# Four-kilobyte pieces for the gate and up weights of a mixture-of-experts layer

## The chip, the core and the metric

The kernel runs on one core of one Trainium2 chip. The metric is the device time of one execution in microseconds (us), as the median of several runs. The core has five engines that each run their own instruction stream in order: TensorE (PE, matrix products; its weight loads are listed apart as PEld), VectorE (DVE), ScalarE (ACT), GpSimd (POOL) and SyncE (SP), which here issues nearly all the transfers from memory. The transfers are carried by 16 DMA engines.

## The reference

256 tokens of width 1024 pass through three layers, all in float32: a layer with forgetting attention and sparse attention, then a mixture of experts, then two hybrid layers (a gated recurrence beside windowed attention). The change is in the mixture of experts:

```python
hid = silu(einsum('td,edf->etf', t, w_gate)) * einsum('td,edf->etf', t, w_up)
hid = hid * combine.T[:, :, None]          # top 2 of 16 experts for each token
y = einsum('etf,efd->td', hid, w_down)
```

There are 16 experts; for each, w_gate and w_up are 1024 x 512 and w_down is 512 x 1024, so 2 MB each.

## The kernel before

The instructions are made by Python generators, and a scheduler in the kernel puts them in an order for each engine before anything runs. It has a cost model of its own (for a DMA: bytes over 360 bytes per ns plus a constant, so the number of bytes counts and not their arrangement) and picks, engine by engine, the task that its model says can start first. Where the model says that PE would stand idle, `keep_warm` puts matmuls on a tile of ones into PE's stream; they write a PSUM tile that nobody reads (`warm` in the rows). They are in the stream once and for all: they run whether or not PE would have had to wait on the chip.

Weights arrive through `loader`. It walks `K.plan`, a list of 1 MB units, takes a free slot (`raw`, 128 partitions x 2048 floats) for each, and lets SP issue its DMAs; at most `K.raw_max` slots are out at a time (`MOE_RAW` = 19 in the expert part). Units of the other layers are then split by ACT and DVE into two halves of lower precision; the expert weights are used as they are (`how == "whole"`).

`plan_moe` makes for each expert four units "gu", each with two chunks of 128 rows of w_gate and the same two of w_up, and two units "d" of w_down. Row number k * 128 + p of the weights lies in partition p, so a partition of a gu unit receives four separate pieces of 512 floats: two of w_gate, two of w_up, side by side with a gate row beside an up row.

`moe` runs one expert after the other. Each expert has room for 64 tokens (`CAP`). For every four experts, `group(q)` gathers their tokens: a matmul per chunk k of 128 columns, with those columns of the tokens as the stationary operand and a 0/1 matrix `Pm` (tile `rows`) as the moving one, gives the chunk's transposed tokens; ACT or DVE scales them by the norm gains `K.gT` into `xt`. The first group (q = 0) takes the tokens `K.x` in full float32. For the other three, `halves()` has split `K.x` once into two parts, `xhl` (tiles `xh` and `xl`): ACT copies the upper part, DVE subtracts. After the gather the expert's eight chunks of gate and up are multiplied (`bank<-raw,xt` in the rows), the product goes through SwiGLU on ACT and DVE (tile `route`), w_down follows (`bank<-raw,route`), and a matmul with the transposed 0/1 matrix (`acc<-rows`) adds the weighted result to the sum for all tokens. `rows_of(e)` makes that transposed matrix: DVE writes two 0/1 tiles (`route<-cp,route`), PE transposes them (`bank<-cp,route`).

`overflow` is a branch that computes all experts for all tokens if some expert has more than 64 tokens; it is not entered with these inputs.

For comparison, one other place reads memory at a distance: `blocks` in the first layer adds a position table to keys of which it reads every 16th element (`cb<-cb`, 64 partitions x 120 elements).

Of the kernel before, what the change touches and what calls it, by code (L numbers as in the profile page):

```python
# [9 lines left out]
F32 = mybir.dt.float32  # L10
# [487 lines left out]
def loader(K, between):  # L498

    nc, sch = K.nc, K.S  # L500
    loaded = [Flag() for _ in K.plan]
    raws = {}

    def load():
        yield ("if", lambda: K.go)
        for i, u in enumerate(K.plan):
            yield ("if", lambda: K.raws < K.raw_max and K.slots.free)
            K.raws += 1
            raw, s = yield from big(K, [128, 2048], "raw")
            rv = raw[:, :u.a * u.n].rearrange("p (a n) -> p a n", a=u.a)  # L510
            for src, c in u.pieces:
                yield nc.sync.dma_start(rv[:, :, c:c + src.shape[2]], src)
            raws[i] = (raw, s, rv)
            loaded[i].done = True
            if i in between:
                yield from between[i]()

    def part(u, i, j, src, sh, w, s):
        wh, wl = (w[:, o:o + sh[0] * sh[1]].rearrange("p (a n) -> p a n", a=sh[0]) for o in (0, 1024))
        yield nc.scalar.activation(wh, src, AF.Copy)  # L520
        yield nc.vector.tensor_sub(wl, src, wh.bitcast(F32))
        u.half[j] = (wh, wl, s)
        u.flag[j].done = True
        if all(f.done for f in u.flag):
            K.raws -= 1
            K.slots.release(raws.pop(i)[1])

    sch.spawn(load(), P_SPLIT)
    for i, u in enumerate(K.plan):
        yield wait(loaded[i])  # L530
        if u.how == "whole":
            u.half = raws.pop(i)
            u.flag[0].done = True
            continue
        rv = raws[i][2]
        for j in range(2):
            yield ("if", lambda: K.halves < K.half_max and K.slots.free)
            K.halves += 1
            w, s = yield from big(K, [128, 2048], "w", F32R)
            if u.how == "col":  # L540
                src, sh = rv[:, :, 128 * j:128 * j + 128], [8, 128]
            else:
                m = u.a // 2
                src, sh = rv[:, m * j:m * j + m, :], [m, u.n]
            sch.spawn(part(u, i, j, src, sh, w, s), P_LATE if u.key[:2] == "wo" else P_SPLIT)
# [171 lines left out]
def split(K, h, l, src):  # L717

    yield K.nc.scalar.activation(h, src, AF.Copy)
    yield K.nc.vector.tensor_sub(l, src, h.bitcast(F32))  # L720
# [583 lines left out]
def plan_moe(K):  # L1304
    I = K.I

    def down(e):
        wr = I["w_down"][0, e].rearrange("(a p) c -> p a c", p=128)
        for u in range(2):
            K.plan.append(Unit("d", [(wr[:, 2 * u:2 * u + 2], 0)], 2, 1024, "whole"))  # L1310
    for e in range(NE):
        for u in range(4):
            wr = [I[nm][0, e].rearrange("(a p) c -> p a c", p=128)[:, 2 * u:2 * u + 2] for nm in ("w_gate", "w_up")]
            K.plan.append(Unit("gu", [(wr[0], 0), (wr[1], 512)], 2, 1024, "whole"))
        if e:
            down(e - 1)
    down(NE - 1)
# [6 lines left out]
def moe(K, edge, done):  # L1324
    nc, I, sch = K.nc, K.I, K.S
    sp = sch.spawn
    ident = K.c("ident")
# [130 lines left out]
    t_half, xhl = [], []  # L1458

    def halves():  # L1460

        for nm in ("xh", "xl"):
            xhl.append((yield from big(K, [128, 2, D], nm, F32R)))
        for t in range(2):
            yield from split(K, xhl[0][0][:, t], xhl[1][0][:, t], K.x[:, t])

    def both(a, b):
        yield wait(a)
# [2 lines left out]
    def group(q):  # L1471

        g = Group()
        p = P_EVAC if q else P_EDGE
        t_one = [sp(one_hot(q, t), p) for t in range(2)]
        g.xt = None
        g.there = [Flag() for _ in range(8)]

        def part(k):
            early = q == 0 and k < 6  # L1480
            yield wait(t_one[0] if early else t_one, t_half if q else None)
            res = K.accs if early and k < 4 else K.banks
            pg, b_ = yield from (acc_tile if res is K.accs else bank)(K, [128, 4, CAP])
            for t in range(2):
                yield wait(t_one[t])
                c = slice(k * 128, k * 128 + 128)
                if q == 0:
                    yield nc.tensor.matmul(pg, K.x[:, t, c], Pm[:, t].bitcast(F32), start=(t == 0), stop=(t == 1))
                for i, x in enumerate(xhl if q else []):
                    yield nc.tensor.matmul(pg, x[0][:, t, c], Pm[:, t], start=(t + i == 0), stop=(t + i == 2))  # L1490
            done_.append(sp(put(k, pg, lambda: res.release(b_)), p))

        def put(k, pg, free):
            yield ("if", lambda: g.xt is not None)
            yield scaled(K, g.xt[:, k], pg, K.gT[:, k:k + 1])
            free()
            g.there[k].done = True
        done_ = []
        ts = [sp(part(k), P_GATHER if q == 0 else p) for k in range(8)]
        g.t_gather = sp(both(ts, done_), p)  # L1500
        if q == 0:
            yield wait(t_mask, edge.tasks)
            K.slots.release(K.s_hh, edge.room[1])
            K.raw_max += 1
        g.xt, g.s_x = yield from big(K, [128, 8, 4, CAP], "xt")
        groups[q] = g
# [61 lines left out]
    for e in range(NE):  # L1568
        q, j = divmod(e, 4)
        if j == 0:  # L1570
            yield ("if", lambda: q in groups)
            g = groups[q]
        t_rows[e] = sp(rows_of(e), P_SIDE)
        pg, b_ = yield from bank(K, [128, 2, 256])
        for u_ in range(4):
            u = take(K, "gu")
            for a in range(2):
                k = 2 * u_ + a
                if j == 0:
                    yield wait(g.there[k])  # L1580
                w = yield from whole(K, u)
                for h in range(2):
                    c = w[:, a].rearrange("p (i f) -> p i f", i=2)[:, :, 256 * h:256 * h + 256]
                    yield nc.tensor.matmul(pg[64 * h:64 * h + 64], g.xt[:, k, j], c, start=(k == 0), stop=(k == 7))
            drop_whole(K, u)
        if j == 3:
            K.slots.release(g.s_x)
            if q < 3:
                sp(group(q + 1), P_EVAC)
        hid[e] = sp(hidden(e, pg, b_), P_EVAC)  # L1590
        if e == 1:
            for i in range(4):
                a = yield from acc_tile(K, [128, 512])
                acc.append(a)
        if e:
            yield from down(e - 1)
            downs[e - 1].done = True
        if e == 2:
            K.raw_max -= 2
            t_half.append(sp(halves(), P_EVAC))  # L1600
        if e == 1:
            K.bounds = sp(bounds(), P_SIDE)
        if e == 10:
            box = []
            yield sch.call(lambda: box.append(nc.real.values_load(
                cmi[0:1, 0:1], min_val=0, max_val=S, skip_runtime_bounds_check_because="a count of tokens")))
            n_max = box[0]
            K.raw_max -= 3
        if e == 12:
            yield wait(groups[3].t_gather)  # L1610
            yield from overflow(K, n_max, combF, comb)
            K.raw_max += 3
        if e == 13:
            K.slots.release(xhl[0][1], xhl[1][1])
            K.raw_max, K.half_max = MOE_END, 8
# [8 lines left out]
def overflow(K, n_max, combF, comb):  # L1624

    tc, nc, I = K.tc, K.nc.real, K.I
# [8 lines left out]
    def body():  # L1635
        with tc.If(n_max > CAP):
# [3 lines left out]
            for k in range(8):  # L1640
                pt = bs[k % 2][0][:, 0:S]
                for t in range(2):
                    nc.tensor.transpose(pt[:, t * 128:(t + 1) * 128], hn[:, t, k * 128:(k + 1) * 128], K.c("ident"))
                nc.vector.tensor_scalar_mul(hT[:, k], pt, K.gT[:, k:k + 1])
            with tc.For_i(0, NE, 1) as e:
                for f in range(4):
                    for i, nm in enumerate(("w_gate", "w_up")):
                        w = raw[:, 1024 * i:1024 * i + 1024].rearrange("p (a c) -> p a c", a=8)
                        nc.sync.dma_start(w, I[nm][0][bass.ds(e, 1), :, f * 128:(f + 1) * 128]
                                          .rearrange("o (a p) c -> p (o a) c", p=128))  # L1650
                        pg = bs[i][0][:, 0:S]
                        for k in range(8):
                            nc.tensor.matmul(pg, w[:, k], hT[:, k], start=(k == 0), stop=(k == 7))
# [402 lines left out]
def tile_kernel(ctx, tc, I, out, parts="am01"):  # L2056
# [20 lines left out]
    def router():  # L2077

        yield ("if", lambda: K.next >= 8 or parts[0] == "m")
        g = I["norm_ffn_g"]  # L2080
        yield nc.gpsimd.dma_start(K.gT, bass.AP(tensor=g.tensor, offset=g.offset, ap=[[1, 128], [128, 8]]))
        yield nc.gpsimd.dma_start(K.w20[:, :, 0:4], I["w_group"][0].rearrange("(a p) c -> p a c", p=128))
        yield nc.gpsimd.dma_start(K.w20[:, :, 4:20], I["w_router"][0].rearrange("(a p) c -> p a c", p=128))
        yield nc.gpsimd.dma_start(K.b20[:, 0:4], bcast_rows(I["b_group"], 4))
# [152 lines left out]
```

## Time and profile before

| | us |
|---|---|
| median of 3 runs (lowest to highest) | 995.18 (995.14 to 996.44) |
| profiled execution, device time | 995.24 |
| its span, first to last instruction | 993.5 |
| PE busy in the span | 979.1 |
| DVE busy | 691.4 |
| ACT busy | 501.2 |
| POOL busy | 28.9 |

The profiled execution is 2 us longer than its span and agrees with the median of the runs. An engine's busy time is an average over very different stages, so it is read by stage: the expert part's first product with expert weights starts 249.5 us into the span and the last one ends near 486 us.

### The profile page before, as it was taken

The numbers are of one execution on the slowest core, as the hardware profiler recorded it, in microseconds if no ns is written. First come the engines' busy times: TensorE is split into PE (matmuls) and PEld (weight loads), VectorE is DVE, ScalarE is ACT, GpSimd is POOL, SyncE is SP. The second block draws the span as 40 slices with busy tenths as digits, with TensorE's granted clock in tenths as the row PEclk, the third lists the DMA queues.
The fourth block names the chain that finished last, engine by engine and source line by source line (L and its number), as shares of the span: only waits on it lengthen the run. The fifth ranks groups of instructions, "written<-read, shape, count | busy, mean of one in ns | idle before, by whom it ended". The sixth has DMA issues, their size and how long they took to land.

```text
span 993.5 us, 16750 instructions
## 1 busy us (share of the span) xinstructions
PE 979.1 (99%) x6385; PEld 750.9 (76%) x6385; DVE 691.4 (70%) x1746; ACT 501.2 (50%) x1070; POOL 28.9 (3%) x67
## 2 busy tenths in 40 slices
PE   9999999999999999999999999999999999999998
PEld 8877999888434343444588989898788898988887
DVE  5778977876355434533687799899858489899952
ACT  5556879842021111110354648687755265867841
POOL 0101000000000000000000000000100000000000
PEclk9999999999999999999999999999999999999999
DMA  8822683798799999999913415432947142443331
GB/s 304 307 69 88 209 304 109 266 343 301 267 393 373 395 392 396 393 386 343 365 36 92 149 58 171 128 125 72 334 129 252 43 128 76 138 129 127 127 107 43
DMA packets 122931, 210.34 MB, mean 212 GB/s; under 512 B 6142, under 2 KB 54512, under 8 KB 122848
## 3 DMA queue, kind: packets, MB, share of 16 engines
q1 hardware_dynamic: 121632, 206.01, 59.2%
q0 software_dynamic: 1216, 3.22, 1.0%
q8 instruction: 52, 0.85, 0.4%
q14 instruction: 31, 0.25, 0.1%
HBM read 208.17 MB, written 1.05 MB: 211 GB/s over the span
## 4 chain that ended last, share of the span: by engine, by line
PE 47%; DVE 6%; DMA 1%; issue 1%; POOL 0%; ACT 0%; DVEq 0%; POOLq 0%
PE acc L202 35%; PE bank L202 11%; DVE ha L202 2%; PE warm L202 1%; DVE ap L202 1%; DMA raw<-in_w_in_dram 1%; DVE hb L202 1%; DVE w L202 1%; DVE og L202 0%; POOL sq L202 0%; DVE tiny L202 0%; DVE x L202 0%; ACT za L202 0%; DVE hn L202 0%; ACT hb L202 0%
## 5 line engine op out<-in xcount | busy, mean ns | idle before, releaser
L202 DVE TENSOR_TENSOR w<-raw,w 128x1024 fp32r<-128x1024 f32 (+1 forms) x196 | 235.3, 1220 | 28.2 <-ACT w L202 27.1
L202 PE MATMUL acc<-hh,w 128*128 128x256 f32 x1280 | 244.2, 287 | 0.0
L202 ACT ACTIVATE w<-raw 128x1024 fp32r<-128x1024 f32 (+1 forms) x196 | 198.7, 1041 | 21.9 <-PE acc L202 11.1
L202 PEld LDWEIGHTS acc<-hh,w 128*128 128x128 f32 x1280 | 201.8, 191 | 3.7 <-issue 1.4
L202 PE MATMUL acc<-hl,w 128*128 128x256 f32 x640 | 184.0, 288 | 0.0
L202 PE MATMUL acc<-w,hh 128*128 128x512 f32 (+2 forms) x512 | 155.2, 380 | 0.0
L202 PEld LDWEIGHTS acc<-hl,w 128*128 128x128 f32 x640 | 122.3, 191 | 3.5 <-issue 1.7
L202 PE MATMUL bank<-raw,xt 128*64 128x512 f32 x512 | 119.4, 600 | 0.0
L202 PEld LDWEIGHTS acc<-w,hh 128*128 128x128 f32 x512 | 92.1, 188 | 16.9 <-issue 2.1
L202 PE MATMUL acc<-w,hl 128*128 128x512 f32 (+2 forms) x256 | 96.5, 377 | 0.0
L202 ACT ACTIVATE route<-bank,route 128x256 f32<-128x256 f32 x16 | 7.6, 474 | 166.2 <-PE bank L202 166.2
L202 PE MATMUL acc<-w,og 128*128 128x512 f32 x384 | 89.1, 391 | 0.0
L202 PEld LDWEIGHTS acc<-w,og 128*128 128x128 f32 x384 | 71.7, 188 | 14.7
L202 PEld LDWEIGHTS bank<-raw,xt 128*64 128x64 f32 x512 | 33.1, 136 | 55.0 <-issue 48.7
L202 DVE TENSOR_TENSOR ha<-ha 128x256 f32<-128x256 f32 (+5 forms) x216 | 71.6, 365 | 4.2 <-PE bank L202 4.0
L202 ACT ACTIVATE ap<-ap,tiny 128x256 f32<-128x256 f32 (+1 forms) x110 | 47.8, 448 | 27.3 <-DVE tiny L202 26.8
L202 PE MATMUL bank<-raw,route 128*64 128x512 f32 x256 | 60.4, 599 | 0.0
L202 PEld LDWEIGHTS warm<-ones 128*128 128x128 f32 x325 | 45.6, 201 | 15.4 <-issue 9.1
L202 PE MATMUL warm<-ones 128*128 128x256 f32 x325 | 54.5, 309 | 2.7 <-ACT ones L424 2.4
L202 PEld LDWEIGHTS acc<-w,hl 128*128 128x128 f32 x256 | 48.3, 189 | 7.3
L202 DVE TENSOR_SCALAR route<-route 128x256 f32<-128x256 f32 (+2 forms) x24 | 6.2, 272 | 57.7 <-ACT route L202 57.6
L202 PEld LDWEIGHTS bank<-raw,route 128*64 128x64 f32 x256 | 16.8, 136 | 28.8 <-issue 25.8
(276 smaller groups left out, 1350.5 us busy)
## 6 DMA issues: line engine op xcount, KB each, us to landing
raw<-in_w_in_dram SPq DMA_DIRECT2D x68, 1024.0 KB, 6.1
raw<-in_w_gate_dram SPq DMA_DIRECT2D x64, 512.0 KB, 10.1
raw<-in_w_up_dram SPq DMA_DIRECT2D x64, 512.0 KB, 10.6
raw<-in_w_down_dram SPq DMA_DIRECT2D x32, 1024.0 KB, 11.9
raw<-in_w_out_dram SPq DMA_DIRECT2D x20, 1024.0 KB, 5.2
raw<-in_cmp_k_w_dram SPq DMA_DIRECT2D x2, 1024.0 KB, 5.8
raw<-in_cmp_v_w_dram SPq DMA_DIRECT2D x2, 1024.0 KB, 5.6
raw<-in_w_fox_up_dram SPq DMA_DIRECT2D x2, 1024.0 KB, 12.2
```

The lines of the kernel that those rows point to most:

```text
L202: go = lambda: f(*a, **k)
```

## The change

Row 8 p + k of w_gate and w_up now lies in partition p as chunk k. Two neighbouring chunks are two neighbouring rows in memory, so a partition of a gu unit receives two pieces of 1024 floats: one of w_gate into the first half of the slot, one of w_up into the second (`how == "pair"`). The product's moving operand takes its 256 gate columns and its 256 up columns at a distance of 1024 floats instead of 512. The tokens' columns must be taken in the same order: chunk k is now every eighth column, starting at k. The first group's gather reads `K.x` so, as its stationary operand; the split writes `xh` and `xl` with the columns already in the new order and reads `K.x` at the distance for it. The gains `K.gT` are loaded in the same order, which makes each partition's eight values neighbours in memory. w_down, the router's weights and everything outside the expert part stay as they are.

```diff
             for src, c in u.pieces:
-                yield nc.sync.dma_start(rv[:, :, c:c + src.shape[2]], src)
+                if u.how == "pair":
+                    yield nc.sync.dma_start(raw[:, c:c + 1024].rearrange("p (a n) -> p a n", a=2), src)
+                else:
+                    yield nc.sync.dma_start(rv[:, :, c:c + src.shape[2]], src)
...
-            wr = [I[nm][0, e].rearrange("(a p) c -> p a c", p=128)[:, 2 * u:2 * u + 2] for nm in ("w_gate", "w_up")]
-            K.plan.append(Unit("gu", [(wr[0], 0), (wr[1], 512)], 2, 1024, "whole"))
+            wr = [I[nm][0, e].rearrange("(p a) c -> p a c", a=8)[:, 2 * u:2 * u + 2] for nm in ("w_gate", "w_up")]
+            K.plan.append(Unit("gu", [(wr[0], 0), (wr[1], 1024)], 2, 1024, "pair"))
...
-            yield from split(K, xhl[0][0][:, t], xhl[1][0][:, t], K.x[:, t])
+            yield from split(K, *(a[0][:, t].rearrange("p (k d) -> p k d", k=8) for a in xhl), K.x[:, t].rearrange("p (d k) -> p k d", k=8))
...
-                    yield nc.tensor.matmul(pg, K.x[:, t, c], Pm[:, t].bitcast(F32), start=(t == 0), stop=(t == 1))
+                    yield nc.tensor.matmul(pg, K.x[:, t, k::8], Pm[:, t].bitcast(F32), start=(t == 0), stop=(t == 1))
...
-                    c = w[:, a].rearrange("p (i f) -> p i f", i=2)[:, :, 256 * h:256 * h + 256]
+                    c = w.rearrange("p i (b f) -> p i b f", b=2)[:, :, a, 256 * h:256 * h + 256]
...
-        yield nc.gpsimd.dma_start(K.gT, bass.AP(tensor=g.tensor, offset=g.offset, ap=[[1, 128], [128, 8]]))
+        yield nc.gpsimd.dma_start(K.gT, bass.AP(tensor=g.tensor, offset=g.offset, ap=[[8, 128], [1, 8]]))
```

The overflow branch's loads and transposes are rewritten in the same way.

The scheduler's order is the same on every engine; only the shapes of the gate and up loads and of the load of `gT` differ. On SP, where the expert weights begin behind the first layer's output weights, the rows stand so (- before, + after):

```order
 L202 DMA raw<-in_w_out_dram 128x4x512 x4
-L202 DMA raw<-in_w_gate_dram 128x2x512
-L202 DMA raw<-in_w_up_dram 128x2x512
-L202 DMA raw<-in_w_gate_dram 128x2x512
-L202 DMA raw<-in_w_up_dram 128x2x512
```

Each of these pairs becomes 128x1024 in its old place; no load has moved. On DVE, around the subtraction that makes `xl`, the rows of before and of the changed kernel are word for word the same:

```order
L202 SCALAR_TENSOR_TENSOR rows<-bank,route,rows 64x512 x2
L202 TENSOR_TENSOR xl<-x,xh 128x1024 x2
L202 TENSOR_SCALAR lbt<-lbt 128x16 x2
L202 TENSOR_SCALAR route<-cp,route 128x128
L202 TENSOR_TENSOR lbt<-lbt 128x16
L202 TENSOR_SCALAR route<-cp,route 128x128
L202 CAST rows<-bank 128x256
```

Nothing moved here either: the two 0/1 tiles of the next expert (`route<-cp,route`) still stand right behind the two subtractions.

## Rows read from the trace of the kernel before

**Rows 1.** The page: span, PE's share, and 40 slices of DMA use and rate
```profile
span 993.5 us, 16750 instructions
...
PE   9999999999999999999999999999999999999998
...
DMA  8822683798799999999913415432947142443331
GB/s 304 307 69 88 209 304 109 266 343 301 267 393 373 395 392 396 393 386 343 365 36 92 149 58 171 128 125 72 334 129 252 43 128 76 138 129 127 127 107 43
```
**Rows 2.** Stretches, from:to and length; busy by engine; PEclk, DMA share, GB/s
```profile
332.00:336.00 4.00, 4.00 (x20) 1.81 (x19) 3.29 (x6) 0.38 (x1) 0.00 (x0) 1.00 1.05 388
340.00:344.00 4.00, 4.00 (x22) 1.26 (x18) 1.26 (x3) 1.31 (x3) 0.00 (x0) 1.00 1.03 408
347.00:353.00 6.00, 6.00 (x32) 2.85 (x30) 2.21 (x7) 0.00 (x0) 0.00 (x0) 1.00 1.05 387
448.00:450.00 2.00, 2.00 (x14) 1.64 (x14) 0.88 (x4) 0.00 (x0) 0.00 (x0) 1.00 0.09 20
```
**Rows 3.** Waits of PE's matmuls, 240 to 500 us: in total, times, longest
```profile
PE bank L202 <- DVE hn L202: 0.7, 1, 0.7
...
PE bank L202 <- PEq L1636: 0.2, 1, 0.2
```
**Rows 4.** PE in order of time: start, length; middle and late experts
```profile
379.33 4.51 PE L202 MATMUL bank<-raw,xt 128*64 128x512 f32 x20
...
392.00 4.51 PE L202 MATMUL bank<-raw,xt 128*64 128x512 f32 x20
...
449.76 1.94 PE L202 MATMUL bank<-raw,xt 128*64 128x512 f32 x8
...
453.93 0.98 PE L202 MATMUL warm<-ones 128*128 128x256 f32 x6
...
467.13 1.94 PE L202 MATMUL bank<-raw,xt 128*64 128x512 f32 x8
469.00 0.50 PE L202 MATMUL warm<-ones 128*128 128x256 f32 x2
469.43 1.94 PE L202 MATMUL bank<-raw,xt 128*64 128x512 f32 x8
```
**Rows 5.** SP's issues in order of time: start, length
```profile
435.25 1.93 SPq L202 DMA_DIRECT2D raw<-in_w_up_dram  x1
448.71 0.38 SPq L202 DMA_DIRECT2D raw<-in_w_gate_dram  x1
```
**Rows 6.** ACT, DVE and PE around the split of the tokens
```profile
289.78 2.01 ACT L202 ACTIVATE xh<-x 128x1024 fp32r<-128x1024 f32 x2
...
291.36 2.36 DVE L202 TENSOR_TENSOR xl<-x,xh 128x1024 fp32r<-128x1024 f32 x2
...
293.79 0.28 DVE L202 TENSOR_SCALAR route<-cp,route 128x128 f32<-128x128 f32 x1
...
294.35 0.33 PE L202 MATMUL bank<-cp,route 128*128 128x128 f32 x1
...
295.62 0.33 PE L202 MATMUL bank<-cp,route 128*128 128x128 f32 x1
```
**Rows 7.** DVE groups by form: count, busy us, mean ns, idle before
```profile
L202 DVE TENSOR_TENSOR w<-raw,w 128x1024 fp32r<-128x1024 f32 x192 | 232.4, 1230 | 26.8 <-ACT w L202 25.8
...
L202 DVE TENSOR_TENSOR cb<-cb 64x120 f32<-64x120 f32 x16 | 5.2, 356 | 0.2
...
L202 DVE TENSOR_TENSOR kv<-kv 128x128 f32<-128x128 f32 x8 | 2.0, 288 | 0.1
```
**Rows 8.** PE in order of time: a gather of the first group, one of the second
```profile
255.16 1.99 PE L202 MATMUL bank<-rows,x 128*128 128x256 f32 x8
...
298.43 0.28 PE L202 MATMUL bank<-rows,xh 128*128 128x256 f32 x1
298.55 0.28 PE L202 MATMUL bank<-rows,xl 128*128 128x256 f32 x1
```

More of the change, by code (lines that the diff above doesn't have):

```diff
@@ L530, in loader @@
         yield wait(loaded[i])
-        if u.how == "whole":
+        if u.how in ("whole", "pair"):
             u.half = raws.pop(i)
@@ L1485, in part @@
                 yield wait(t_one[t])
-                c = slice(k * 128, k * 128 + 128)
+                c = slice(128 * k, 128 * k + 128)
                 if q == 0:
-                    yield nc.tensor.matmul(pg, K.x[:, t, c], Pm[:, t].bitcast(F32), start=(t == 0), stop=(t == 1))
+                    yield nc.tensor.matmul(pg, K.x[:, t, k::8], Pm[:, t].bitcast(F32), start=(t == 0), stop=(t == 1))
                 for i, x in enumerate(xhl if q else []):
@@ L1642, in body @@
                 for t in range(2):
-                    nc.tensor.transpose(pt[:, t * 128:(t + 1) * 128], hn[:, t, k * 128:(k + 1) * 128], K.c("ident"))
+                    nc.tensor.transpose(pt[:, t * 128:(t + 1) * 128], hn[:, t, k::8], K.c("ident"))
                 nc.vector.tensor_scalar_mul(hT[:, k], pt, K.gT[:, k:k + 1])
@@ L1649, in body @@
                         nc.sync.dma_start(w, I[nm][0][bass.ds(e, 1), :, f * 128:(f + 1) * 128]
-                                          .rearrange("o (a p) c -> p (o a) c", p=128))
+                                          .rearrange("o (p a) c -> p (o a) c", a=8))
                         pg = bs[i][0][:, 0:S]
```

## The prediction

> **What bounds the kernel now.** I read the page's slices first. In the expert part (the 12th to the 20th slice lie wholly in it or nearly so) the DMA engines are busy nearly throughout at 343 to 396 GB/s, and PE is at 9 in every slice [rows 1]. Both look like the limit there, so the slices don't decide it. The table of stretches tells which gives way. While w_down arrives in pieces of 4 KB the rate is 408 GB/s; while w_gate and w_up arrive in pieces of 2 KB it is 387 to 388 GB/s, at the same share of busy time [rows 2]. So the longer pieces do move faster, by 5%, and the question is only whether anyone waits for them.
>
> The waits say no. Between 240 and 500 us PE's matmuls waited four times, 0.7 us at most and 0.2 us at least, and none of the four was for a DMA [rows 3]. The order of time says why. In the middle of the part an expert takes PE 12.67 us (379.33 to 392.00) without a gap; near the end it takes 17.37 us (449.76 to 467.13), with matmuls on ones in between [rows 4]. An expert's 6.29 MB take 16.0 us at about 394 GB/s (between the two rates of [rows 2]). So in the middle PE eats a stock of loads that were issued ahead, and near the end PE runs at the slower pace that the scheduler wrote into its stream, whether the data are there or not. The stock never runs out: from 448 to 450 us the DMA engines are 9% busy [rows 2], so the load issued at 435.25 [rows 5] has landed by then, and it is the last expert's second unit of gate and up, which PE reads at 467.13 [rows 4]. That is a lead of at least 17 us; the third unit, issued at 448.71, is read at 469.43. PE's stream is the bound of this part, and it hands each delay on to the end, since none of the four waits is long enough to swallow one.
>
> **The change, part by part.** *The loads.* 64 gate and 64 up DMAs keep their bytes, their place on SP and their semaphores, and go from pieces of 2 KB to 4 KB. The 67.1 MB take 173.0 us of DMA time at 388 GB/s and 164.5 us at 408, so 8.5 us of DMA time go. The cover is complete: a lead that is 17 us or more only grows, and the matmuls on ones stay in the stream. Counted: 0. The loads of the layer behind, which queue behind the last w_down, come at most by a share of that earlier; the splits that use them stand in DVE's and ACT's streams behind work on PE's last products, so again 0.
>
> *The moving operand.* The same two runs of 256 floats per matmul, farther apart. Before, too, the runs lay apart, and 20 passes took 4.51 us wherever they stood together [rows 4]; the passes read the same floats in the same runs, so both ends are 0.
>
> *The gains.* One small load by POOL, hundreds of us before its use: 0.
>
> *The split.* Two ACT copies (2.01 us together) and two DVE subtractions (2.36 us together) now read `x` at a distance of 8 floats [rows 6]. The trace has no such read of a large tile. The nearest row is `cb<-cb`, 120 elements of which one input is read at every 16th float: 356 ns. Plain DVE subtractions and additions give 288 ns for 128 elements and 1230 ns for 1024, so 1.05 ns per element and 153 ns fixed, and 120 plain elements would take 279 ns [rows 7]. The distance costs 77 ns there, 0.64 ns per element; for 1024 elements 0.66 us. From below I bound it by 0 (a read at a distance has no reason to be faster), from above by twice that on both engines. I take 0.66 us per instruction on DVE, and the same on ACT, for which no row exists.
>
> The chain then goes so. ACT's copies end at about 291.5 and 293.1 instead of 290.8 and 291.8; DVE's subtractions, from 291.36 on, run into 295.25 instead of 293.72, so 1.5 us later. Behind them on DVE stand the two 0/1 tiles of the next expert; the first ended at 294.07 (293.79 + 0.28) and PE transposes it at 294.35 [rows 6]. PE, in order, has less than 0.28 us to spare there. It would wait about 1.3 us. The second transpose, at 295.62, moves along and finds its tile ready. With ACT at no extra cost the delay is 1.3 - 0.3 = 1.0 us, with twice the cost on both engines DVE ends near 297.1 and PE waits some 3.1 us. Everything behind on PE (products, ones, the other layers) moves by the same amount, and with them what SP and DVE do, since these wait for PE. Counted: +1.3 us, ends 0 and 3.1.
>
> [...]
>
> *The first gather.* 8 chunks, two token halves, two passes each in float32: 32 weight loads from `x` at a distance of 8 floats. The 8 passes of two chunks take 1.99 us, so about 0.22 us a pass [rows 8]. In the second group a pass with its load follows the one before by 0.12 us (298.43 to 298.55) [rows 8], so a plain load of 128 columns needs no more than 0.12 us and hides behind the pass before it. At DVE's 0.64 ns per element a load grows by 0.08 us to 0.20 us: still hidden, except where a chunk's first load has no pass to hide behind, at most 8 times 0.08 = 0.7 us. I take half, +0.35 us; ends 0 and, with loads at three times 0.12 us, 32 x 0.14 = 4.5 us.
>
> *Sum*, against the profiled execution (span 993.5 us, 995.24 us with what lies around it, 0.06 above the median): 995.24 + 0 + 1.3 + 0.35 = 996.9, and beside the median of 995.18 that is 996.8.
>
> **The rivals.** *The loads were the limit after all.* For it: DMA busy throughout, and its rate is 5% better with long pieces. Then up to 8.5 us would come back: 986.7 us. Against: no DMA among PE's waits, the lead of 17 us, and ones in the stream late in the part.
>
> [...]
>
> *Weight loads at a distance outgrow the passes* (slower). The place is the first gather, 247 to 262 us, where PE has nothing else to do than these passes and the first products. It decides from the point where a load takes more than 0.22 us, so nearly twice a plain one. At three times: 995.2 + 4.5 + 1.3 = 1001.0 us. For it: 128 separate reads per partition, and DVE shows that such reads cost. Against: by DVE's figure a load stays at 0.20 us.
>
> *The long pieces come slower* (slower). A load now takes 4 KB out of every 16 KB of memory, where before it took 256 KB in one run. If the gate and up traffic, two thirds of the 171 us from 275 to 446, took 30% longer, that would be 34 us, less the lead of 17: about 1012 us. It begins to count once the pieces are 15% slower. Against: w_down's 4 KB pieces are the fastest here.
>
> *Reads at a distance cost nothing* (the change does nothing for the time): 995.2 us. For it only that no row has this very shape.
>
> **How the numbers follow.** A measurement of this kernel tells about 0.2%, 2 us, from no change: 993.2 to 997.2 counts as the same. Forecast 0.64, of which I put a bit over a quarter above 997.2, since its two terms have ends of 3.1 and 0.7 us and the middle lies close to that line. Reads at no cost 0.16. Weight loads outgrow the passes 0.10. Loads were the limit 0.05. Long pieces slower 0.05. So faster 0.06 (the first rival and a little scatter), same 0.61 (0.46 of the forecast, 0.15 of the free reads), slower 0.33 (0.18 of the forecast, 0.10 and 0.05). The predicted time is 996.8 us. The range goes from 994.8, the free reads with the scatter of runs, to 999.5, the forecast's upper part and the first steps of outgrown loads; out of it lie the two extreme rivals and about half of the outgrown loads.
>
> **What would show it.** Gate and up stretches at about 408 GB/s and a DMA that idles more around 446 us: the loads step is right. `xl<-x,xh` near 1.9 us instead of 1.2 and `xh<-x` near 1.7, with an idle time of PE ahead of the transpose at 294 us that names DVE's `route`: the split step is right, and from there on the same shift in every stage. The eight passes `bank<-rows,x` still at about 2.0 us: the gather step is right; at 2.5 or more the second rival is. The forecast is wrong if PE's time for an expert changes, if a wait of PE names a DMA, or if the shift at 294 us is gone again at 490 us.

## The result: slower by half a per cent

| | before | changed |
|---|---|---|
| median of 5 runs each, us (lowest to highest) | 996.06 (995.14 to 996.48) | 1001.08 (1000.57 to 1002.03) |
| profiled execution: device time, us | 995.24 | 1002.03 |
| its span, us | 993.5 | 1000.3 |
| mean granted clock of TensorE in the five runs | 1.0 in the profiled one | 0.996 to 0.998 |

The ratio is 1.0053, 95% interval 1.0039 to 1.0067: slower, by more than the 0.2% that a measurement of this kernel tells. The prediction was 996.8 us with a range to 999.5.

The page of the changed kernel, the lines that answer to [rows 1] and the one on packets:

```profile
span 1000.3 us, 16750 instructions
...
PEclk9999999999998999999999999999999999999999
...
GB/s 304 300 72 88 214 294 121 284 330 295 252 393 296 408 409 409 409 382 356 356 25 85 127 85 135 126 123 84 329 154 252 43 127 59 153 127 127 125 107 43
DMA packets 106547, 210.34 MB, mean 210 GB/s; under 512 B 6142, under 2 KB 54512, under 8 KB 106464
```

The transfers did what the change meant: 408 to 409 GB/s in the 14th to 17th slice, where before it was 392 to 396 [rows 1]. But the 13th slice has a granted clock that is not full, and the rate falls to 296 GB/s in the same slice. Stretches of the changed kernel (from:to and length; busy time of PE, PEld, DVE, ACT, POOL; granted clock, DMA share, GB/s), the first two against [rows 2]:

```profile
347.00:353.00 6.00, 6.00 (x30) 1.91 (x28) 2.86 (x6) 1.69 (x4) 0.00 (x0) 1.00 1.03 411
448.00:450.00 2.00, 2.00 (x13) 0.79 (x9) 1.19 (x3) 0.14 (x1) 0.00 (x0) 1.00 0.33 133
...
296.00:299.00 3.00, 1.07 (x5) 0.34 (x5) 2.27 (x6) 0.00 (x0) 0.00 (x0) 0.92 1.02 401
299.00:302.00 3.00, 3.00 (x11) 1.33 (x9) 0.79 (x4) 0.00 (x0) 0.00 (x0) 0.50 0.59 176
302.00:305.00 3.00, 3.00 (x9) 0.75 (x6) 0.37 (x2) 0.17 (x1) 0.00 (x0) 0.50 0.72 283
305.00:310.00 5.00, 5.00 (x30) 3.10 (x31) 1.90 (x5) 2.45 (x6) 0.00 (x0) 0.97 0.60 213
```

From 299 to 305 us TensorE has a granted clock of 0.50, where the kernel before has 1.00 in the same stretches. What it did before shows in its order of time, to be read beside [rows 6] and [rows 8]:

```profile
256.26 2.29 PE L202 MATMUL bank<-rows,x 128*128 128x256 f32 x8
258.48 1.08 PE L202 MATMUL bank<-raw,xt 128*64 128x512 f32 x4
...
294.17 1.94 PE L202 MATMUL bank<-raw,xt 128*64 128x512 f32 x8
298.04 0.33 PE L202 MATMUL bank<-cp,route 128*128 128x128 f32 x1 [1.93 <-DVE route L202]
298.30 1.82 PE L202 MATMUL bank<-raw,xt 128*64 128x512 f32 x4
300.06 0.47 PE L202 MATMUL bank<-cp,route 128*128 128x128 f32 x1
...
301.11 3.68 PE L202 MATMUL bank<-raw,xt 128*64 128x512 f32 x8
304.71 0.58 PE L202 MATMUL bank<-rows,xh 128*128 128x256 f32 x1
...
473.95 1.94 PE L202 MATMUL bank<-raw,xt 128*64 128x512 f32 x8
```

PE waited 1.93 us for DVE's 0/1 tile, as the prediction said it would (it said 1.3). Right behind the wait four passes take 1.82 us, and eight take 3.68 where eight took 1.94 ahead of it. Who was late is on ACT and DVE:

```profile
291.47 4.14 ACT L202 ACTIVATE xh<-x 128x1024 fp32r<-128x1024 f32 x2
...
293.60 4.04 DVE L202 TENSOR_TENSOR xl<-x,xh 128x1024 fp32r<-128x1024 f32 x2 [0.58 <-ACT xh L202]
...
297.71 0.28 DVE L202 TENSOR_SCALAR route<-cp,route 128x128 f32<-128x128 f32 x1
```

ACT's two copies went from 2.01 to 4.14 us, DVE's two subtractions from 2.36 to 4.04 [rows 6], and DVE now also waits for ACT.

Where the 6.8 us of span between the two profiled executions went can be read by setting PE's rows side by side. The first gather starts 0.5 us later (247.13 before, 247.59 after). That is start-up, whose length varies from run to run: in the six experiments below whose scheduler's model is the same, the first gather starts between 247.28 and 249.90 us. The first product behind the split's wait, the transpose, stands at 298.04 instead of 294.35 [rows 6], 3.7 us later: 0.5 of start-up, 1.2 us of gather, 2.0 us of wait. The first pass of the second group's gather stands at 304.71; before, the row is

```profile
298.09 0.39 PE L202 MATMUL bank<-rows,xh 128*128 128x256 f32 x1
```

so it comes 6.6 us later, and the 2.9 us since the transpose are the half clock. From there on the shift hardly moves: 473.95 for the 467.13 of [rows 4] is 6.8, and at the end of the span it is 6.8. In the medians the changed kernel is 5.0 us slower; the profiled execution is the slowest of the five.

### The profile page after: what moved, and what is told of

Its sections match the earlier page's. It is cut to its first block, busy times and chain, and to the rows that moved or that the text cites. A ratio compares the mean times of both kernels' runs of the same rounds, so it can differ in the third digit from the quotient of the medians.

```text
span 1000.3 us, 16750 instructions
## 1 busy us (share of the span) xinstructions
PE 983.8 (98%) x6385; PEld 754.5 (75%) x6385; DVE 693.1 (69%) x1746; ACT 503.4 (50%) x1070; POOL 28.6 (3%) x67
## 3 DMA queue, kind: packets, MB, share of 16 engines
HBM read 208.17 MB, written 1.05 MB: 209 GB/s over the span
## 4 chain that ended last, share of the span: by engine, by line
PE 49%; DVE 6%; issue 0%; POOL 0%; ACT 0%; DVEq 0%
PE acc L202 35%; PE bank L202 12%; PE warm L202 2%; DVE ha L202 2%; DVE ap L202 1%; DVE hb L202 1%; DVE w L202 1%; POOL sq L202 0%; DVE og L202 0%; DVE tiny L202 0%; DVE rows L202 0%; DVE x L202 0%; ACT za L202 0%; DVE hn L202 0%; ACT hb L202 0%
## 5 line engine op out<-in xcount | busy, mean ns | idle before, releaser
L202 PE MATMUL bank<-raw,xt 128*64 128x512 f32 x512 | 121.9, 611 | 0.0
```

The costliest lines, as they stand in the source:

```text
L202: go = lambda: f(*a, **k)
```

## The experiments

Each is the kernel before or the changed one with a small edit. All were timed beside runs of the kernel before on the same chip.

**The loads alone.** The kernel before with the long pieces; gather and split read `x` plainly. The amount of work is the same, but the tokens' columns no longer belong to the weights' rows; the same holds, for some of the experts, of the next two kernels.

```diff
-            yield from split(K, *(a[0][:, t].rearrange("p (k d) -> p k d", k=8) for a in xhl), K.x[:, t].rearrange("p (d k) -> p k d", k=8))
+            yield from split(K, xhl[0][0][:, t], xhl[1][0][:, t], K.x[:, t])
...
-                    yield nc.tensor.matmul(pg, K.x[:, t, k::8], Pm[:, t].bitcast(F32), start=(t == 0), stop=(t == 1))
+                    yield nc.tensor.matmul(pg, K.x[:, t, c], Pm[:, t].bitcast(F32), start=(t == 0), stop=(t == 1))
```

(The diff is against the changed kernel.)

> Only the new arrangement of the gate and up loads and of the products' moving operand is kept; the gather and the split of the tokens read x as before, so the experts get tokens whose columns don't match the weights' rows. My theory (the strided reads of x cost the time, the loads nothing): 995.2 to 996.4 us, the same as the kernel before; PE clock 1.0 throughout; gate and up stretches at about 408 GB/s. Rival (the new loads or the wider distance in the moving operand cost the time): about 1001 us, with PE slower per expert or waiting for a DMA.

Measured: 996.12 us against 995.89, ratio 1.0004 (0.9995 to 1.0013), granted clock 1.0 in the profiled execution. One of the eleven runs took 998.20 us with a mean clock of 0.998; it was not traced. A stretch of gate and up loads that had 388 GB/s [rows 2]:

```profile
332.00:336.00 4.00, 4.00 (x19) 1.70 (x19) 3.46 (x6) 0.38 (x1) 0.00 (x0) 1.00 1.03 407
```

So the pieces of 4 KB move 5% faster and change the time by nothing that can be measured. The loads step of the prediction holds, and the loss lies in the reads of `x`.

**The split plain**, the gather still at a distance (the first half of the diff above alone).

> The changed kernel, but the split reads x plainly, so the parts for the second to fourth group have the old column order. My theory: the wait of 1.9 us at 298 us and the fall of the clock behind it are gone, the slower gather of the first group (1.1 us) stays: 996.3 to 997.5 us, clock 1.0. Rival (the slower gather is the larger part): 1000 us or more.

Measured: 997.08 us, ratio 1.0011 (1.0002 to 1.0020), against the same 995.89. PE of this kernel, the gather and the transpose that waited:

```profile
257.02 2.29 PE L202 MATMUL bank<-rows,x 128*128 128x256 f32 x8
...
296.79 0.33 PE L202 MATMUL bank<-cp,route 128*128 128x128 f32 x1
```

No wait ahead of the transpose and no fall of the clock. Eight passes take 2.29 us instead of 1.99 [rows 8]; there are four such groups of eight, so the gather costs 1.2 us, and that is what the medians show. (The transpose stands 2.4 us later than before: the other 1.2 us are start-up, since the first gather starts at 248.34 instead of 247.13.)

**The gather plain**, the split still at a distance (the second half of that diff alone).

> The changed kernel, but the first group's gather reads x plainly, so the first four experts get the old column order. My theory: PE's wait of about 1.9 us for DVE and the 6.8 us at half clock behind it stay, the gather's 1.1 us go: 999.8 to 1001 us. Rival (gather is the larger part): below 998 us.

Measured: 1000.67 us, ratio 1.0042 (1.0028 to 1.0055). PE of its profiled execution, then the stretches of the same place:

```profile
297.45 0.33 PE L202 MATMUL bank<-cp,route 128*128 128x128 f32 x1 [1.95 <-DVE route L202]
...
299.35 3.55 PE L202 MATMUL bank<-raw,xt 128*64 128x512 f32 x8
```
```profile
299.00:302.00 3.00, 3.00 (x13) 1.10 (x11) 1.16 (x4) 0.00 (x0) 0.00 (x0) 0.54 0.78 273
302.00:305.00 3.00, 3.00 (x17) 1.23 (x13) 0.69 (x2) 1.36 (x4) 0.00 (x0) 0.89 0.59 201
```

The same wait, and again a half clock behind it, here for about half as long as in the changed kernel. The eight runs fall into two sets: three with a mean granted clock of 1.0 took 997.24, 997.46 and 998.49 us, five with 0.996 to 0.998 took 999.98 to 1001.84. One program, one order, the same data: in the first set the time is above the kernel before by about the length of the wait (997.46 less 995.89 is 1.6), in the second by 2.5 to 4.4 us more. Only one of the eight was traced, so where the clock fell in the other four, and how often, is not shown. The median of the five, 1001.57, is 5.7 us above the kernel before, more than the changed kernel's 5.0 although the gather's 1.2 us are not in it; the price of the falls varies by more than the gather costs.

**The wait filled.** The changed kernel with 16 matmuls on ones in PE's stream ahead of the waiting transpose:

```diff
-            yield nc.tensor.transpose(p2[:, t * 128:(t + 1) * 128], dup[:, t], ident)
+            o = nc.tensor.transpose(p2[:, t * 128:(t + 1) * 128], dup[:, t], ident)
+            if e == 3 and t == 0:
+                go = o.alts[0][3]
+
+                def with_ones(go=go):
+                    for _ in range(16):
+                        nc.real.tensor.matmul(p2[:, 0:256], K.one_r, K.one_r[:, None, :].to_broadcast([128, 2, 128]), start=True, stop=True)
+                    return go()
+                o.alts = [o.alts[0][:3] + (with_ones,)]
+            yield o
```

> The changed kernel with 16 matmuls on ones put on PE right ahead of the transpose that waits, about 1.9 us of work where PE stood idle. My theory (the wait makes the clock fall, and the low clock costs another 3.1 us): the clock stays at 1.0 and the time is 997.8 to 999.2 us, so 2 to 3 us better than the changed kernel although nothing is taken from the path. Rival (the clock falls for another reason, or the slow stretch has another cause): 1001 us or more with the clock still 0.5 for some us.

Measured: 999.69 us (998.81 to 1000.11), ratio 1.0038 (1.0025 to 1.0051). PE, and one of the stretches that had 0.50:

```profile
295.88 2.17 PE L1461 MATMUL bank<-ones 128*128 128x256 f32 x16
298.00 0.33 PE L202 MATMUL bank<-cp,route 128*128 128x128 f32 x1
...
299.87 1.94 PE L202 MATMUL bank<-raw,xt 128*64 128x512 f32 x8
```
```profile
299.00:302.00 3.00, 3.00 (x17) 1.34 (x16) 1.16 (x4) 0.15 (x1) 0.00 (x0) 1.00 0.75 264
```

The transpose starts no sooner (DVE is as late as it was), but the clock stays at 1.00, the eight passes take 1.94 us, and all five runs have a mean clock of 1.0. So in these traces the fall goes with the idle time ahead of the transpose (1.93 us idle and 0.50 behind it in the changed kernel, none idle and 1.00 here), not with the late tile as such. The medians agree only roughly: this kernel is 3.8 us above the runs of the kernel before that were timed with it, the changed kernel 5.0 above its own, and the two intervals overlap; 999.69 also lies above the 997.8 to 999.2 that were expected. The 3.8 us fit the gather (1.2), the late tile (2.1 in the trace) and leave 0.5, which is within what start-up varies by. The clock rows carry the verdict here, not the difference of the times.

**The split out of the way.** The changed kernel with each split cut into four pieces of 256 columns and a lower priority in the scheduler, which puts the 0/1 tiles ahead of most of them:

```diff
-            yield from split(K, *(a[0][:, t].rearrange("p (k d) -> p k d", k=8) for a in xhl), K.x[:, t].rearrange("p (d k) -> p k d", k=8))
+            x3 = [a[0][:, t].rearrange("p (k d) -> p k d", k=8) for a in xhl] + [K.x[:, t].rearrange("p (d k) -> p k d", k=8)]
+            for k in range(0, 8, 2):
+                yield from split(K, *(a[:, k:k + 2] for a in x3))
...
-            t_half.append(sp(halves(), P_EVAC))
+            t_half.append(sp(halves(), P_LATE))
```

> The changed kernel, all of it, with the split cut into eight pieces and given a lower priority, so that the two 0/1 tiles of the next expert come before most of it on VectorE. My theory (only PE's wait for these two tiles and the low clock behind it are lost to the split): no wait of PE at the transposes near 295 us, clock 1.0, 996.5 to 997.7 us, so 1.1 us over the kernel before for the gather. Rival (the split's length has to be paid somewhere, at the second group's gather near 299 us at the latest): a wait of 1 us or more there and 998.5 us or more.

Measured: 996.63 us against 995.53, ratio 1.0009 (1.0000 to 1.0018), clock 1.0. DVE's order of time in this kernel:

```profile
293.67 0.64 DVE L202 TENSOR_TENSOR xl<-x,xh 128x256 fp32r<-128x256 f32 x1
294.21 0.48 DVE L202 TENSOR_SCALAR route<-cp,route 128x128 f32<-128x128 f32 x2
294.60 3.25 DVE L202 TENSOR_TENSOR xl<-x,xh 128x256 fp32r<-128x256 f32 x6
```

The subtractions take no less time than in the changed kernel (4.5 us in all against 4.0), but six of the eight now stand behind the 0/1 tiles, and PE waits for nothing there. What is left, 1.1 us, fits the gather's 1.2. The split's reads at a distance cost nothing that can be measured here: their price was where they stood.

**The writes at a distance instead.** The split walks `x` in its own order and writes `xh` and `xl` at a distance of 128 floats; the subtraction also reads `xh` at that distance:

```diff
-            yield from split(K, *(a[0][:, t].rearrange("p (k d) -> p k d", k=8) for a in xhl), K.x[:, t].rearrange("p (d k) -> p k d", k=8))
+            yield from split(K, *(a[0][:, t].rearrange("p (k d) -> p d k", k=8) for a in xhl), K.x[:, t].rearrange("p (d k) -> p d k", k=8))
```

> The changed kernel with the split's operands walked in the order of x: x is read plainly, and the two parts are written at a distance of 128 floats (the subtraction also reads the upper part at that distance). Theory 1 (a write at a distance costs as much as a read): the copies stay at 2.1 us, the subtractions at 2.0 us or more, 1000 to 1002 us. Theory 2 (writes are free): copies 1.05 us, subtractions about 2.0 us, PE's wait 1.4 us instead of 1.9, 998.5 to 1000.5 us.

Measured: 998.91 us, ratio 1.0033 (1.0020 to 1.0047). ACT and DVE, and then PE's transpose:

```profile
293.78 3.83 ACT L202 ACTIVATE xh<-x 128x1024 fp32r<-128x1024 f32 x2
```
```profile
295.83 3.82 DVE L202 TENSOR_TENSOR xl<-x,xh 128x1024 fp32r<-128x1024 f32 x2 [0.51 <-ACT xh L202]
```
```profile
300.04 0.33 PE L202 MATMUL bank<-cp,route 128*128 128x128 f32 x1 [1.63 <-DVE route L202]
```

The copies alone show a write at a distance of 128 floats: 2.02 us each, about what the read at 8 floats cost (2.12). The subtractions, 1.95 us each, have a read and a write at 128 floats, so they don't tell the two apart. The rows are those of the expectation's first theory, though the time lies in the range of the second. The wait was 1.63 us, and no half clock follows it in this trace; gather (1.2) and wait (1.7 by the shift of the transpose) make 2.9 of the median's 3.4 us.

Yet the profiled execution has a mean clock of 0.998 and is 2 us above the median. Its fall of the clock stands elsewhere, near the start, in the first layer:

```profile
17.45 0.39 PE L202 MATMUL warm<-ones 128*128 128x256 f32 x1 [1.77 <-DVE hl L202]
```
```profile
20.00:22.00 2.00, 2.00 (x6) 1.58 (x5) 2.00 (x3) 0.38 (x2) 0.00 (x0) 0.50 1.11 308
```

PE waited 1.77 us there for a tile of DVE, ran at half clock from about 19.4 to 22.7 us, and the first gather starts at 249.90 us, 2.8 later than in the kernel before. The edits don't touch this work, and the wait varies by itself: in the other traces it is between nothing (the kernel before and the changed one) and 1.4 us (the plain split), and no half clock follows it. So a mean clock below 1.0 does not tell which wait it belongs to; that takes a trace.

**What the faster loads are worth once they are planned for.** Three kernels have 400 instead of 360 bytes per ns for the expert weights in the scheduler's model, so that fewer matmuls on ones are put between the late experts (260 in all instead of 325 in the kernel before): the kernel before, the kernel with the split out of the way, and the loads alone.

```diff
-            cost = int(np.prod(aps[0].shape)) * 4 / 360.0 + (1 if eng == "SP" else 20)
+            fast = aps[1].tensor.name in ("in_w_gate_dram", "in_w_up_dram", "in_w_down_dram")
+            cost = int(np.prod(aps[0].shape)) * 4 / (400.0 if fast else 360.0) + (1 if eng == "SP" else 20)
```

> The kernel before, with 400 instead of 360 bytes per ns for the expert weights in the scheduler's cost model; 65 fewer matmuls on ones stand in PE's stream. My theory (PE's stream with its ones is the bound of the expert part, the loads are 17 us ahead): 985 to 988 us, with about 7 us of lead left and no wait of PE for a DMA. Rival (the loads are close enough to be the bound once PE is faster): 991 us or more, with PE waiting for gate and up loads.

> The changed kernel with the split behind the two 0/1 tiles, and 400 instead of 360 bytes per ns in the cost model. My theory: the same gain as the kernel before has from that, plus the 1.1 us of the gather: 986 to 989.5 us, so 0.5 to 2 us slower than the kernel before with 400. Rival (with the ones gone the faster loads count): faster than the kernel before with 400 by 2 us or more.

Measured: the kernel before with 400 took 990.57 us, ratio 0.9948 (0.9934 to 0.9961); the changed one with the split out of the way and 400 took 986.12, ratio 0.9901 (0.9886 to 0.9916). The first fits neither figure of its expectation well, and the second beat the first by 4.4 us, as the rival of its expectation had it and not the theory. The trace of the kernel before with 400 says why. ACT, then PE and a stretch behind its wait:

```profile
471.90 2.00 ACT L203 ACTIVATE w<-raw 128x1024 fp32r<-128x1024 f32 x2 [4.15 <-DMA raw<-in_w_in_dram]
473.81 0.67 ACT L203 ACTIVATE rows<-bank,route 64x512 fp32r<-64x512 f32 x1
```
```profile
474.80 3.68 PE L203 MATMUL bank<-raw,route 128*64 128x512 f32 x8 [4.51 <-ACT route L203]
```
```profile
475.00:478.00 3.00, 3.00 (x8) 0.56 (x6) 2.80 (x4) 2.98 (x4) 0.00 (x0) 0.50 1.05 382
```

ACT, in order, waits 4.15 us for a weight of the next layer, whose load queues behind the last w_down; the expert's own work stands behind that copy, PE waits 4.5 us for it, and runs the eight passes behind the wait at half clock (3.68 us). This wait of PE names ACT, and yet a DMA is the cause. (The one PE wait of the expert part that names a DMA is 0.7 us, for a small load, `lbsrc`.) That the long pieces alone take this away, and not the place of the split, was put to a test with the third kernel:

> The kernel before with the long pieces alone (gather and split read x plainly, so the columns of x and of the weights don't belong together; the work is that of before), and with 400 instead of 360 bytes per ns for the expert weights in the scheduler's model. The order is that of the kernel before with 400, which took 990.6 us and waited 4.5 us for ACT's route at 470 us, while ACT stood behind a copy w<-raw that waited 4.1 us for a DMA of the next layer. Theory: the long pieces let that DMA land some 3 us earlier, so that ACT is in time and PE neither waits nor loses its full clock there; without the gather's and the split's reads at a distance this gives 984.5 to 986 us, a PE wait on ACT's route under 1 us, and granted clock 1.0 throughout. Rival: the 4.4 us between the two kernels with 400 came from where the split stood and not from the pieces; then this kernel waits about 4.5 us again and takes 989 to 991 us.

Measured: 984.46 us, ratio 0.9886 (0.9869 to 0.9902), clock 1.0. (As in the loads alone, columns and rows don't belong together.) The same places:

```profile
467.18 1.99 ACT L203 ACTIVATE w<-raw 128x1024 fp32r<-128x1024 f32 x2
469.08 0.67 ACT L203 ACTIVATE rows<-bank,route 64x512 fp32r<-64x512 f32 x1
```
```profile
470.06 1.94 PE L203 MATMUL bank<-raw,route 128*64 128x512 f32 x8 [0.25 <-ACT route L203]
```

ACT's copy finds its data there, PE waits 0.25 us instead of 4.51, and the passes take 1.94 us. With one and the same order of the work the long pieces are worth 990.57 - 984.46 = 6.1 us, of which 4.3 are the wait and the rest fits the clock. The version with the split out of the way, 986.12 us, beats the kernel before by 9.4 us and the changed one by 15; it still pays 1.7 us more than this last kernel, and the gather's reads cost 1.2 in the experiments above.

## Why the prediction was wrong

The two places where the change costs time, the split and the first gather, were named; the terms there were too small, and a third cost behind the split, the fall of the clock, was not in the forecast at all. The sum was 1.65 us and the medians show 5.0. (Of the 4.3 us between 996.8 and 1001.08, 0.9 is the base: 995.18 in three runs of the kernel before, 996.06 in five.) With the gather's 1.2 and the wait's 2.0 the sum would have been 3.2 us and the time 998.4, inside the range; the clock took it out. By its steps:

- *What bounds the kernel; the loads, 0.* Right: loads alone 1.0004, the rate 407 GB/s there and 411 in the changed kernel, no wait of PE for a DMA.
- *The split, +1.3 with ends 0 and 3.1.* The place, the waiting transpose and the engine waited for were as forecast; the size was 1.93 us. Taking DVE's 77 ns for 120 elements [rows 7] as a measure was near on DVE: (2060 - 1222) ns over 1024 elements is 0.82 ns per element instead of 0.64. On ACT, which had no row, it was (2124 - 1049) over 1024, 1.05 instead of 0.64, and DVE waits for ACT's first part: 0.58 us of ACT's excess were handed on, beside 1.68 of DVE's own.
- *The gather, +0.35 with ends 0 and 4.5.* Measured 1.2, all of it the mechanism of the second rival: the step that failed is "at DVE's 0.64 ns per element a load grows by 0.08 us to 0.20 us: still hidden". The records of the loads from `x` went from 0.19 to 0.33 us, so by 0.145 and not 0.08, and 8 passes from 1.99 to 2.29 us. The pace of the passes was also misread: what follows the 8 passes of [rows 8] in the kernel before is

```profile
257.08 1.08 PE L202 MATMUL bank<-raw,xt 128*64 128x512 f32 x4
```

so they take 1.92 us from start to start, 0.24 us each and not the 0.22 from which the rival was to decide. In the changed kernel it is 2.22 us (256.26 to 258.48), 0.28 each: the loads pass the point by little. The forecast took the weight load's growth from another engine's row, as an estimate; the kernel before had no row at a distance for PE's loads (now 0.33 us) or ACT's copies (now 2.12 us).
- *Behind the wait, nothing.* This is the step that failed most: "Everything behind on PE (products, ones, the other layers) moves by the same amount". That handed a wait on one to one. The wait also brought a fall of the granted clock from 1.0 to 0.5, which no term, end or rival had. In the changed kernel's profile the fall cost 3.1 us (shift 3.7 at the transpose, 6.8 behind it). Over the five runs, 5.0 less 1.2 of gather and 2.0 of wait leaves about 1.8. That it comes with the wait is shown by the filled wait, by the plain split and by the split out of the way: mean clock 0.999 or 1.0 in every run, and 1.00 in the stretches of their traces. A low mean clock alone is no proof of it, since one run of the loads alone, which has no such wait, also had 0.998, and the far writes had their fall in the first layer. In which runs the fall comes, and why it sometimes lasts half as long, stays open.
- *The rivals.* The outgrown loads were the nearest in time (1001.0 against 1001.08) by luck: their own price was 1.2 of the 4.5 us. Reads at a distance are not free; the plain split and the plain gather show a price for either (2.29 against 1.99 us for eight passes of the gather, 4.14 against 2.01 us for ACT's two copies). Long pieces came faster, not slower (411 against 387 GB/s). That the loads were the limit was wrong for this change, but the loads do set a limit close by: with fewer ones in the stream they count, by way of the next layer's weights and ACT (6.1 us between the two kernels with 400). "So again 0" for these weights was right only as long as the ones kept PE slow.
- Of the signs named, the eight passes at 2.29 us lie between the one for the forecast (2.0) and the one for the rival (2.5). The DMA engines should idle more around 446 us; the rows from 448 to 450 are no test of it, since PE and with it the issues were 6.8 us later there. The loads alone, whose PE is not late, can be set beside the kernel before: there the engines are busy for 0.19 and 0.16 of the stretches 442 to 444 and 444 to 446 us, before for 0.47 and 0.09 of 446 to 448 and 448 to 450. The idle time comes some 4 us sooner, which is the faster loads, with nobody waiting for them.

## What to carry to other kernels

When a change makes a busy PE wait anywhere, price the wait and, apart from it, a possible stretch at half clock behind it: here, in both traces that have a wait of 1.9 us with nothing to fill it, some 3.4 and 6.8 us at a granted clock of 0.50 followed, and in other runs of one of these programs the mean clock stayed at 1.0. A new layout that suits the transfers (here 407 against 388 GB/s) moves the distance into every reader of the other operand; find the readers that stand in order ahead of something PE needs, and put them behind it (here a ratio of 1.0009 to the kernel before instead of 1.0053). Where filler work was planned for a slower transfer, faster transfers gave nothing here (996.12 us against 995.89) until the plan was told of them (984.46 against 990.57).

## What the runs showed of the hardware that was not expected

Reads at every eighth float, from the groups by form of the stretch 240 to 500 us (count, busy us, mean ns of one, idle before), first of the kernel before, then of the changed one:

```profile
L202 PEld LDWEIGHTS bank<-rows,x 128*128 128x128 f32 x16 | 2.9, 189 | 1.9 <-issue 1.6
...
L202 DVE TENSOR_TENSOR xl<-x,xh 128x1024 fp32r<-128x1024 f32 x2 | 2.4, 1222 | 0.0
L202 ACT ACTIVATE xh<-x 128x1024 fp32r<-128x1024 f32 x2 | 2.0, 1049 | 0.0
```
```profile
L202 ACT ACTIVATE xh<-x 128x1024 fp32r<-128x1024 f32 x2 | 4.1, 2124 | 0.0
L202 DVE TENSOR_TENSOR xl<-x,xh 128x1024 fp32r<-128x1024 f32 x2 | 4.0, 2060 | 0.6 <-ACT xh L202 0.6
...
L202 PEld LDWEIGHTS bank<-rows,x 128*128 128x128 f32 x16 | 4.0, 334 | 1.6 <-issue 1.6
```

- ACT's copy takes twice as long (2124 against 1049 ns), DVE's subtraction (one of two inputs at the distance) 1.7 times (2060 against 1222), a weight load of 128 columns 1.8 times by its records (334 against 189). With ACT's outputs written at a distance of 128 floats instead, two copies took 3.83 us; two subtractions that wrote and read so took 3.82 (the rows of that experiment).
- In the traces, waits of PE of 1.77, 1.93, 1.95 and 4.51 us were followed or accompanied by a half clock; waits of 1.37 us (start-up, plain split) and 1.63 us (far writes) were not, nor was the one of 2.40 us that opens the span of the kernel before and of the changed one. The length alone does not decide: of eight runs of the program with the wait of 1.95 us in its trace, three had a mean clock of 1.0 and five 0.996 to 0.998.
